# A transformer kernel on one core: the scheduler's stated step durations for DVE, ACT and PE set to measured ones

## The chip, the cores and the metric

The kernel runs on one core of one Trainium2 chip. A core has five engines that run in parallel, each through its own list of instructions in order: TensorE (PE, matrix products; PEld is its loading of weights), VectorE (DVE), ScalarE (ACT), GpSimd (POOL) and SyncE (SP, which here only issues DMAs). They wait for one another by semaphores. The metric is the device time of one execution in microseconds (us); lower is better.

## The reference

The program is two transformer blocks on 512 tokens of width 1024, in float32. The first has two layers, each with a mixer and a SwiGLU feed-forward part (width 2816), with RMS norms before and after. Layer 0 mixes by dilated band attention (12 heads), layer 1 by a gated DeltaNet (6 heads, forward and backward in time); both attend to 256 memory tokens too. The second block has three mixers side by side (GLA, S5, NSA) and one output projection. Cut to what matters:

```python
for i in range(2):
    h = rms_norm(x, pre[i]);  mem_n = rms_norm(mem, mem_norm[i])
    mixed = attention(h, mem_n, ...) if i == 0 else deltanet(h, mem_n, ...)
    x = x + rms_norm(mixed, post[i])
    h = rms_norm(x, ffn_pre[i])
    gate, up = split(h @ w_gate_up[i])
    x = x + rms_norm((silu(gate) * up) @ w_down[i], ffn_post[i])
proj = rms_norm(x, g) @ w_in
x = x + concat(gla(proj), s5(proj), nsa(proj)) @ w_out

# inside deltanet, per head and direction, chunk after chunk:
v_new = u - w @ state
out   = (q * exp(g)) @ state + intra @ v_new
state = state * exp(g_last) + (k * exp(g_last - g)).T @ v_new
```

## The kernel before

**Products.** Each float32 product is made of three matmuls on halves: an operand A is split into a high part Ah, rounded by ACT, and a low part Al = A - Ah, made by DVE; `mm3` (L267) issues low x high, high x low and high x high (lines L271, L272, L273), for each of eight slices of 128 of the inner width. These three lines, with output `bk`, are most of PE's work; "fill matmuls" here means those of them that stand between other work.

**Weights.** `weight_stream` (L216) brings each piece of weights by a DMA on SP's queue (L207) into one of three raw buffers, ACT makes `wh` (L243) and DVE makes `wl` (L262); for some pieces ("aside") POOL makes `wl`. A raw buffer is free again after its `wl`.

**Stages.** At the start the tokens x and the memory are read in tiles of 128 rows (L318), normed (L336 to L346: ACT's sum of squares, DVE's `iss`, POOL's root `irs` L340, DVE's scaled `hs` L346), transposed by PE (`hT` L354) and split (`Xh` L384, `Xl` L386). Then come layer 0's attention, whose last steps broadcast weights by PE (`fbc` L764), scale the output `oT` on DVE (L769) and split it for the output projection (`Xh` L794, `Xl` L796); its feed-forward part; layer 1's DeltaNet; its feed-forward part; and the second block.

**DeltaNet.** For each head an inverse is made by products on 64 columns (up to L1566, result `Uf` L1571). Then two chains, forward and backward, go over four chunks (`chain`, L1580): PE multiplies the state `St` (L1594), DVE makes `rhs` (L1597), PE multiplies by `Uf` (L1602), ACT reads `vn` (L1605), DVE scales it to `vs` (L1610), PE multiplies `vs` (L1612), DVE makes the next `St` (L1616, the first one by a copy L1619); outputs are two matmuls (L1624, L1625) and go to `otok`. When a head's two chains have ended, its output is normed (ACT L1651, POOL L1658), transposed (`poT` L1335), gated (`oT` L1661), and split for the projection (L1706, L1708).

**The order of the work** is made while the program is built, by a small list scheduler, `Flow` (L52 to L148). Every stage is written as threads, Python generators that yield an engine and a stated duration for each step and then issue its instructions. `Flow.start` gives the time at which a step could begin: when its engine is free and its inputs are there, plus `HOP` = 0.2 us where an input comes from another engine. `Flow.run` takes the step that could begin first; among those of the same engine that could begin within 0.1 us it takes the one with the lowest `late`. Tokens passed through `get` and `put` model the buffers. The stated durations are used for nothing else: they decide the order of instructions on each engine, and nothing at run time. Durations come from `act(n)` = 0.1 + 0.00084 n (L155), `dve(n)` = 0.07 + 0.00105 n (L159), `pool(n)` (L163), `MM` and `TR` (L152), or a number at the step:

```python
s = max(s, at + (self.HOP if e != eng else 0.0 if e == "PE" else 0.07))
```

Of the kernel before, what the change touches and what calls it, by code (L numbers as in the profile page):

```python
# [55 lines left out]
class Flow:  # L56
# [5 lines left out]

    HOP = 0.2

    def __init__(self, **sets):
# [33 lines left out]
    def run(self):  # L99
        while self.threads:  # L100
# [40 lines left out]
            s, t = min((x for x in ops if x[1]["req"][0] == t["req"][0] and x[0] <= s + DELTA), key=lambda x: x[1]["late"])  # L141
            eng, cost = t["req"][:2]
            self.free[eng] = s + cost
            t["tok"] = (s + cost, eng)
# [18 lines left out]
class K:  # L163
# [132 lines left out]
    def inputs(self, F, W, eX, eM, eF, pro):  # L296
# [93 lines left out]
        def memory():  # L390
            yield "late", 0.5
            for l in range(2):
                yield "wait", *eN[l]
                for c in range(2):
                    ev = W["mk"][l][c]
                    yield "wait", ev
                    yield "get", "mm"
                    p = self.psum("mm")
                    w = ev["W"]
                    for k in range(KT):  # L400
                        t = yield "PE", 0.33
                        self.mm3(p[:, :256], (w.h[:, k, :], w.l[:, k, :]), (M[l].h[:, k, :], M[l].l[:, k, :]),
                                 k == 0, k == KT - 1)
                    F.put("wsl", t)
                    F.add(evac(self.memK[l][:, c, :], p), 0.5, t)
                yield "wait", *W["mv"][l]
                for u in range(2):
                    yield "get", "mm"
                    p = self.psum("mm")
                    ts = slice(u * P, (u + 1) * P)  # L410
                    for k in range(KT):
                        w, kk = W["mv"][l][k // 4]["W"], k % 4
                        t = yield "PE", 0.33
                        self.mm3(p[:, :256], (M[l].h[:, k, ts], M[l].l[:, k, ts]), (w.h[:, kk, :], w.l[:, kk, :]),
                                 k == 0, k == KT - 1)
                    F.add(evac(self.memV[l][:, u, :], p, l == 1 and u == 1), 0.5, t)
                for _ in range(2):
                    F.put("wsl", t)
# [120 lines left out]
    def attention(self, F, W, eX, eM, eB, at, e2):  # L539
# [41 lines left out]
        def group(g):  # L581
# [37 lines left out]
            for i, t0 in enumerate((0, 64, 192, 320, 384)):  # L619
                yield "get", "mm"  # L620
                p = self.psum("mm")
                for k in range(KT):
                    w, kk = W2[k // 4]["W"], k % 4
                    t = yield "PE", 0.33
                    self.mm3(p[:, :256], (X.h[:, k, t0:t0 + P], X.l[:, k, t0:t0 + P]), (w.h[:, kk, :], w.l[:, kk, :]),
# [396 lines left out]
    def out_ffn(self, F, i, W, gnext, groups, kev, before):  # L1022
# [57 lines left out]
        for part, (f0, f1) in enumerate(self.PARTS):  # L1080
# [22 lines left out]
            while f < nf:  # L1103
                fs = (f, f + 1) if part == 0 and f == 0 else (f,)
                banks = {}
                for hv in ((0, 256), (256, 512)) if len(fs) == 2 else ((0, 512),):
# [3 lines left out]
                    for f_ in fs:  # L1110
                        for z in range(2):
# [6 lines left out]
                            for k in range(KT):  # L1118
                                tk = yield "PE", 0.65 * (t1 - t0) / 512
                                self.mm3(p[:, t0:t1], (ev["W"].h[:, k, :], ev["W"].l[:, k, :]),  # L1120
# [649 lines left out]
    def proj(self, F, ev, eX, m=P):  # L1770
# [7 lines left out]
        for t0, t1 in rngs:  # L1778
            yield "wait", *eX[t0 // P:t1 // P]
            for k in range(KT):  # L1780
                t = yield "PE", 0.65 * (t1 - t0) / S
                self.mm3(p[:m, t0:t1], (W.h[:, k, :], W.l[:, k, :]), (X.h[:, k, t0:t1], X.l[:, k, t0:t1]),
# [5 lines left out]
    def projector(self, F, items, eX, eP, late=20, haste=0):  # L1788
# [9 lines left out]
        def part(it, t0, t1):  # L1798
            W, m = it["W"], it["args"][4]
            yield "wait", *eX[t0 // P:t1 // P]  # L1800
            for k in range(KT):
                t = yield "PE", 0.65 * (t1 - t0) / S
                self.mm3(it["p"][:m, t0:t1], (W.h[:, k, :], W.l[:, k, :]), (X.h[:, k, t0:t1], X.l[:, k, t0:t1]),
# [15 lines left out]
        for i, it in enumerate(items):  # L1819
# [13 lines left out]
            for u in range(4):  # L1833
# [4 lines left out]
                for k in range(KT):  # L1838
                    W, kk = it[k // 4]["W"], k % 4
                    t = yield "PE", 0.33  # L1840
                    self.mm3(p[:, :256], (X.h[:, k, sl], X.l[:, k, sl]), (W.h[:, kk, :], W.l[:, kk, :]),
# [394 lines left out]
    def s5(self, F, W, eX, open_, eY, uT):  # L2236
# [140 lines left out]
        def glu():  # L2377
# [14 lines left out]
            for c in range(2):  # L2392
                zs = []
                for o in (2, 0):
# [3 lines left out]
                    for k in range(2):  # L2398
                        t = yield "PE", 0.65
                        self.mm3(p, (w.h[:, k, os_], w.l[:, k, os_]), yh[k], k == 0, k == 1)  # L2400
# [898 lines left out]
```

## Time and profile before

| | us |
|---|---|
| median of 3 runs (1761.16 to 1765.25) | 1763.18 |
| the profiled execution | 1761.48 |
| its span, first to last instruction | 1759.5 |
| PE busy | 1708.7 (97%) |
| DVE busy | 979.8 (56%) |
| ACT busy | 763.2 (43%) |
| POOL busy | 338.0 (19%) |

The profile is of one execution. An engine's busy time is the time in which it had an instruction in work, waits not counted; PE's matmuls overlap, so two that start 0.23 us apart may each be shown 0.4 us long. In a timeline a row gives the start, the length, the engine, the line of the kernel, the operation, output <- inputs, the size and a count xN of like instructions drawn together; in brackets stands how long the engine had been idle before it, and which instruction released it. Order listings, below, show the instructions of one engine in program order and hold no times.

### The profile page before, as it was taken

Reading aid. Unit: us, or ns where it says so; the run is one execution under the profiler, and the core shown is the slowest. Engines: PE = TensorE matmul, PEld = TensorE weight load, DVE = VectorE, ACT = ScalarE, POOL = GpSimd, SP = SyncE. Lnnn points to the kernel's source line nnn. Section 1 sums busy time; section 2 is a strip of 40 time slices with the busy share of each in tenths; the row PEclk is TensorE's granted clock in tenths of the full one; section 3 lists DMA queues with packets and bytes.
Section 4 is the critical chain, followed back from the end, with each engine's and each line's share of the span. In section 5 each row is a group of like instructions: output and inputs, shape, how many; then the busy total and the mean of one; then the engine's idle time right before and its main releaser. Section 6 shows DMA issues by size and latency. Waiting matters only on the chain.

```text
span 1759.5 us, 30190 instructions
## 1 busy us (share of the span) xinstructions
PE 1708.7 (97%) x12031; PEld 1423.2 (81%) x12031; DVE 979.8 (56%) x1997; ACT 763.2 (43%) x1808; POOL 338.0 (19%) x496
## 2 busy tenths in 40 slices
PE   6999999999999999999999899999999999999999
PEld 5988679888888888788777788888888888888787
DVE  6333656323333378867887467464433468467573
ACT  5443635333223245656555355333223353345671
POOL 5200001000000021220222351364540033210000
PEclk9999999999999999999999999999999999999999
DMA  6513133333233332211110164345333253552012
GB/s 195 154 51 95 49 120 97 120 96 96 96 96 96 96 114 79 61 38 38 38 37 32 59 152 139 109 133 144 108 108 96 77 159 115 153 154 69 25 37 84
DMA packets 211981, 167.84 MB, mean 95 GB/s; under 512 B 21996, under 2 KB 183036, under 8 KB 211840
## 3 DMA queue, kind: packets, MB, share of 16 engines
q1 hardware_dynamic: 203808, 154.39, 29.7%
q0 software_dynamic: 4560, 9.42, 2.1%
q10 hardware_dynamic: 3472, 2.10, 0.4%
q8 instruction: 94, 1.54, 0.4%
q14 instruction: 47, 0.39, 0.1%
HBM read 152.23 MB, written 13.65 MB: 94 GB/s over the span
## 4 chain that ended last, share of the span: by engine, by line
PE 84%; DVE 9%; ACT 2%; issue 2%; DMA 1%; POOL 1%; ACTq 0%; SPq 0%; DVEq 0%; POOLq 0%
PE bk L271 23%; PE bk L272 22%; PE bk L273 22%; DVE hn L1324 2%; DVE wl L262 1%; PE no L2753 1%; PE npT L2736 1%; PE x L1519 1%; PE x L1523 1%; PE y L1544 1%; DVE hs L942 1%; PE ns L2722 1%; PE hT L949 1%; PE ns L2720 1%; PE o L1625 1%
## 5 line engine op out<-in xcount | busy, mean ns | idle before, releaser
L262 DVE TENSOR_TENSOR wl<-raw,wh 128x512 fp32r<-128x512 f32 x450 | 315.8, 742 | 372.4 <-ACT wh L243 371.8
L243 ACT ACTIVATE wh<-raw 128x512 fp32r<-128x512 f32 x474 | 273.0, 623 | 534.4 <-PE bk L273 300.4
L271 PE MATMUL bk<-Xh,wl 128*128 128x512 f32 (+2 forms) x1312 | 494.9, 377 | 0.2 <-ACT Xh L951 0.2
L272 PE MATMUL bk<-Xl,wh 128*128 128x512 f32 (+2 forms) x1312 | 478.4, 365 | 0.5 <-DVE Xl L956 0.5
L273 PE MATMUL bk<-Xh,wh 128*128 128x512 f32 (+2 forms) x1312 | 478.5, 365 | 0.0
L273 PEld LDWEIGHTS bk<-Xh,wh 128*128 128x128 f32 (+1 forms) x1312 | 246.9, 188 | 40.1
L271 PEld LDWEIGHTS bk<-Xh,wl 128*128 128x128 f32 (+1 forms) x1312 | 247.5, 189 | 39.0 <-issue 3.5
L272 PEld LDWEIGHTS bk<-Xl,wh 128*128 128x128 f32 (+1 forms) x1312 | 247.7, 189 | 34.8 <-DVE Xl L956 0.9
L271 PE MATMUL bk<-wh,Xl 128*128 128x512 f32 (+1 forms) x424 | 152.6, 360 | 6.7 <-DVE Xl L796 3.7
L272 PE MATMUL bk<-wl,Xh 128*128 128x512 f32 (+1 forms) x424 | 145.8, 344 | 0.3 <-DVE wl L262 0.2
L273 PE MATMUL bk<-wh,Xh 128*128 128x512 f32 (+1 forms) x424 | 145.2, 342 | 0.0
L271 PE MATMUL bk<-wh,Al 128*128 128x512 f32 x352 | 139.7, 397 | 0.0
L272 PE MATMUL bk<-wl,Ah 128*128 128x512 f32 x352 | 139.5, 396 | 0.0
L921 POOL TENSOR_TENSOR nc<-ncm,nhalf 128x1 f32<-128x1 f32 x16 | 11.5, 720 | 661.9 <-DVE ncm L919 661.9
L273 PE MATMUL bk<-wh,Ah 128*128 128x512 f32 x352 | 138.6, 394 | 0.0
L1093 DVE TENSOR_TENSOR sg<-sg,bk 128x512 f32<-128x512 f32 x44 | 30.2, 687 | 124.7 <-PE bk L273 120.2
L271 PEld LDWEIGHTS bk<-wh,Xl 128*128 128x128 f32 x424 | 84.7, 200 | 18.0 <-DVE Xl L796 3.1
L273 PEld LDWEIGHTS bk<-wh,Xh 128*128 128x128 f32 x424 | 84.8, 200 | 8.1
L272 PEld LDWEIGHTS bk<-wl,Xh 128*128 128x128 f32 x424 | 85.0, 200 | 7.6 <-DVE wl L262 1.0
L271 PEld LDWEIGHTS bk<-wh,Al 128*128 128x128 f32 x352 | 66.0, 188 | 16.1
L273 PEld LDWEIGHTS bk<-wh,Ah 128*128 128x128 f32 x352 | 66.0, 188 | 16.0
L272 PEld LDWEIGHTS bk<-wl,Ah 128*128 128x128 f32 x352 | 66.1, 188 | 15.4
(586 smaller groups left out, 2623.8 us busy)
## 6 DMA issues: line engine op xcount, KB each, us to landing
raw<-in_ffn_w_gate_up_dram SPq DMA_DIRECT2D x88, 512.0 KB, 3.9
raw<-in_ffn_w_down_dram SPq DMA_DIRECT2D x44, 512.0 KB, 3.3
raw<-in_dn_w_in_dram SPq DMA_DIRECT2D x27, 512.0 KB, 4.0
raw<-in_att_w_in_dram SPq DMA_DIRECT2D x20, 512.0 KB, 4.1
raw<-in_w_in_dram SPq DMA_DIRECT2D x20, 512.0 KB, 3.8
raw<-in_mem_w_kv_dram SPq DMA_DIRECT2D x8, 512.0 KB, 3.6
raw<-in_att_w_out_dram SPq DMA_DIRECT2D x8, 512.0 KB, 3.3
xd<-x SPq DMA_DIRECT2D x8, 512.0 KB, 2.6
```

The lines of the kernel that those rows point to most:

```text
L243: nc.scalar.activation(wh[:, sl], ev["raw"][:, sl], AF.Copy)
L262: eng.tensor_tensor(wl[:, sl], raw[:, sl], wh[:, sl].bitcast(F32), op=OP.subtract)
L271: mm(out, A[1], B[0], start=first, stop=False, **kw)
L272: mm(out, A[0], B[1], start=False, stop=False, **kw)
L273: mm(out, A[0], B[0], start=False, stop=last, **kw)
L942: nc.vector.scalar_tensor_tensor(hh[:, hv[i]], x[:, t, hv[i]], r2, r["gain"][:, hv[i]], op0=OP.mult, op1=OP.mult)
L949: nc.tensor.transpose(p[:, k * P:(k + 1) * P], hh[:, i * 512 + k * P:i * 512 + (k + 1) * P], self.ident)
L1093: nc.vector.tensor_tensor(sg, sg, pu, op=OP.mult)
L1324: nc.vector.scalar_tensor_tensor(acc[:, d0:d1], raw[:, d0 + o:d1 + o], cw[:, ti, tap:tap + 1], acc[:, d0:d1], op0=OP.mult, op1=OP.add)
L1519: nc.tensor.matmul(dn8(b[i])[at], lhsT, rhs, start=True, stop=True)
L1523: nc.tensor.transpose(b[d][:, o:o + P], U[:, d, 2 * n:2 * n + 2, :].rearrange("p c q -> p (c q)"), self.ident)
L1544: nc.tensor.matmul(dn8(ys[par])[HB[f], d, n, :], T[d][HB[par], n, f, :], xs[f][HB[par], d, n, :], start=True, stop=True)
```

## The change

`Flow` adds a fixed amount to the stated duration of every step on DVE (0.08 us) and on ACT (0.07 us). The steps that issue one `mm3` state 0.36 us in the place of 0.33 for 256 columns, and 0.682 in the place of 0.65 for 512. No instruction's arithmetic changes: each engine issues the same instructions in another order, apart from loads of ACT's function tables, which follow from the order of ACT's functions: there are 7 where there were 11. In the new file lines are one or two further down. Of the eight places with a PE number two are shown.

```diff
@@ -61,6 +61,7 @@
 
 
     HOP = 0.2
+    STEP = {"DVE": 0.08, "ACT": 0.07}
 
     def __init__(self, **sets):
         self.free = dict.fromkeys(("PE", "ACT", "DVE", "POOL", "DMA"), 0.0)
@@ -140,6 +141,7 @@
             s, t = min(ops, key=lambda x: x[0])
             s, t = min((x for x in ops if x[1]["req"][0] == t["req"][0] and x[0] <= s + DELTA), key=lambda x: x[1]["late"])
             eng, cost = t["req"][:2]
+            cost += self.STEP.get(eng, 0.0)
             self.free[eng] = s + cost
             t["tok"] = (s + cost, eng)
             self.step(t, t["tok"])
@@ -398,7 +400,7 @@
                     p = self.psum("mm")
                     w = ev["W"]
                     for k in range(KT):
-                        t = yield "PE", 0.33
+                        t = yield "PE", 0.36
                         self.mm3(p[:, :256], (w.h[:, k, :], w.l[:, k, :]), (M[l].h[:, k, :], M[l].l[:, k, :]),
                                  k == 0, k == KT - 1)
                     F.put("wsl", t)
...
@@ -1116,7 +1118,7 @@
                                 banks[f_, z] = self.psum("bk"), nm
                             p = banks[f_, z][0]
                             for k in range(KT):
-                                tk = yield "PE", 0.65 * (t1 - t0) / 512
+                                tk = yield "PE", 0.682 * (t1 - t0) / 512
                                 self.mm3(p[:, t0:t1], (ev["W"].h[:, k, :], ev["W"].l[:, k, :]),
                                          (X.h[:, k, t0:t1], X.l[:, k, t0:t1]), k == 0, k == KT - 1)
                             if t1 == S:
...
```

**POOL at the start.** `irs` is the root of a tile's norm (two memory tiles, then four x tiles), `wl` the low half of memory weights, `rb` and `oh` are small inputs. Before:

```order
L340 TENSOR_TENSOR irs<-iss,nhalf 128x1 x2
L444 MEMSET rb 33x12
L446 DMA oh<-in_bucket_oh_dram 33x1152
L448 DMA rb<-in_rel_bias_dram 32x12
L340 TENSOR_TENSOR irs<-iss,nhalf 128x1
L262 TENSOR_TENSOR wl<-raw,wh 128x512 x3
L340 TENSOR_TENSOR irs<-iss,nhalf 128x1
L262 TENSOR_TENSOR wl<-raw,wh 128x512 x2
L340 TENSOR_TENSOR irs<-iss,nhalf 128x1
L262 TENSOR_TENSOR wl<-raw,wh 128x512 x2
```

After:

```order
L342 TENSOR_TENSOR irs<-iss,nhalf 128x1 x2
L446 MEMSET rb 33x12
L448 DMA oh<-in_bucket_oh_dram 33x1152
L450 DMA rb<-in_rel_bias_dram 32x12
L342 TENSOR_TENSOR irs<-iss,nhalf 128x1 x3
L264 TENSOR_TENSOR wl<-raw,wh 128x512 x2
L342 TENSOR_TENSOR irs<-iss,nhalf 128x1
L264 TENSOR_TENSOR wl<-raw,wh 128x512 x2
```

Before, each of the x tiles' `irs` stands behind a group of `wl` steps, three long at first; now three `irs` steps come one after the other ahead of the first `wl` steps. On SP's queue the four x tiles are now fetched one after the other, while before the third and the fourth stood behind pieces of weights; in PE's order the first transposes of x stand behind 24 memory matmuls where there were 45, the last behind 48 where there were 123.

**PE at the end of attention.** `ao` is the attention's output, `fbc` the broadcast of the groups' weights, `bk` the fill matmuls. Before:

```order
L706 MATMUL ao<-pT,V_882 64x128 x4
L764 MATMUL fbc<-ident,amx 64x128 x6
L271 MATMUL bk<-wh,Xl 128x512
L272 MATMUL bk<-wl,Xh 128x512
L273 MATMUL bk<-wh,Xh 128x512
L271 MATMUL bk<-wh,Xl 128x512
L272 MATMUL bk<-wl,Xh 128x512
L273 MATMUL bk<-wh,Xh 128x512
L764 MATMUL fbc<-ident,amx 64x128 x18
```

After:

```order
L273 MATMUL bk<-wh,Xl 128x512
L274 MATMUL bk<-wl,Xh 128x512
L275 MATMUL bk<-wh,Xh 128x512
L273 MATMUL bk<-wh,Xl 128x512
L274 MATMUL bk<-wl,Xh 128x512
L275 MATMUL bk<-wh,Xh 128x512
L273 MATMUL bk<-wh,Xl 128x512
L274 MATMUL bk<-wl,Xh 128x512
L275 MATMUL bk<-wh,Xh 128x512
L766 MATMUL fbc<-ident,amx 64x128 x12
L273 MATMUL bk<-wh,Xl 128x512
L274 MATMUL bk<-wl,Xh 128x512
```

Before, six broadcasts stand right behind the `ao` matmuls, then six fill matmuls, then the other eighteen, and the output projection. Now twelve fill matmuls stand behind the `ao` matmuls (the first three just ahead of the rows shown), and the twelve last broadcasts behind them, followed by 129 fill matmuls up to the projection's later steps, where there were 123.

**PE in the last head of DeltaNet**, in the middle of its two chains; `chain`, `o` and the names in them are those of the code, the numbers tell buffers apart. Before:

```order
L1594 MATMUL chain<-St_9699,kTh 128x128
L1624 MATMUL o<-St_9664,qe_9081 128x128
L1625 MATMUL o<-vn_9693,AT_9055 128x128
L271 MATMUL bk<-wh,Xl 128x512
L272 MATMUL bk<-wl,Xh 128x512
L273 MATMUL bk<-wh,Xh 128x512
L1602 MATMUL chain<-rhs_9715,Uf 128x128
L1594 MATMUL chain<-St_9710,kTh 128x128
L271 MATMUL bk<-wh,Xl 128x512
L272 MATMUL bk<-wl,Xh 128x512
L273 MATMUL bk<-wh,Xh 128x512
L1602 MATMUL chain<-rhs_9729,Uf 128x128
```

After:

```order
L1596 MATMUL chain<-St_9737,kTh 128x128
L1596 MATMUL chain<-St_9742,kTh 128x128
L1604 MATMUL chain<-rhs_9751,Uf 128x128
L1604 MATMUL chain<-rhs_9753,Uf 128x128
L1614 MATMUL chain<-vs_9761,ktok 128x128
L1614 MATMUL chain<-vs_9763,ktok 128x128
L1626 MATMUL o<-St_9737,qe_9143 128x128
L1627 MATMUL o<-vn_9757,AT_9070 128x128
L1626 MATMUL o<-St_9742,qe_9255 128x128
L1627 MATMUL o<-vn_9759,AT_9229 128x128
```

Before, blocks of three fill matmuls stand between the chains' links: from the last head's inverse (the last L1566) to its transposes `poT` there are 54 in all, 6 ahead of the first link, 33 in eleven blocks between the links, and 15 behind the last link. Now there are none from the inverse to `poT`, and the two chains' links stand side by side. All 54 stand ahead of that inverse now: counted from the start of the program, fill matmuls ahead of the six heads' inverses are 9, 15, 36, 45, 48 and 54 more than before.

## Rows read from the trace of the kernel before

**Rows 1.** The page's busy times: engine, us, share of the span, instructions.

```profile
PE 1708.7 (97%) x12031; PEld 1423.2 (81%) x12031; DVE 979.8 (56%) x1997; ACT 763.2 (43%) x1808; POOL 338.0 (19%) x496
```

**Rows 2.** Busy time by stretches: start:end, length, each engine's busy time, PE's clock, DMA.

```profile
core 0: us, PE busy (x) PEld busy (x) DVE busy (x) ACT busy (x) POOL busy (x), PEclk, DMA share, GB/s
0.00:45.00 45.00, 30.46 (x173) 26.00 (x174) 28.34 (x41) 25.79 (x48) 25.64 (x33) 0.92 0.66 193
200.00:240.00 40.00, 33.02 (x281) 24.64 (x280) 30.00 (x75) 21.52 (x72) 0.00 (x0) 0.96 0.09 28
700.00:740.00 40.00, 38.18 (x500) 29.80 (x499) 32.07 (x67) 25.72 (x59) 11.35 (x9) 1.00 0.20 54
740.00:844.70 104.70, 104.11 (x1276) 84.96 (x1274) 77.61 (x187) 60.13 (x169) 19.66 (x18) 1.00 0.16 42
844.70:983.00 138.30, 130.22 (x1716) 107.57 (x1716) 107.74 (x243) 75.70 (x214) 34.83 (x28) 0.98 0.12 36
983.00:998.80 15.80, 15.80 (x106) 13.92 (x104) 9.38 (x28) 5.35 (x16) 0.00 (x0) 1.00 0.00 1
998.80:1010.00 11.20, 8.05 (x34) 6.10 (x33) 3.45 (x7) 3.96 (x15) 8.70 (x13) 0.90 0.38 126
1010.00:1410.00 400.00, 399.16 (x1876) 331.48 (x1875) 205.91 (x424) 143.08 (x277) 149.83 (x288) 1.00 0.42 119
1470.00:1730.00 260.00, 258.06 (x2155) 213.03 (x2154) 166.95 (x372) 135.16 (x369) 28.44 (x30) 1.00 0.32 91
```

**Rows 3.** Timeline of the start: start, length, engine, line, operation, [idle before <- releaser].

```profile
21.06 0.68 DVE L262 TENSOR_TENSOR wl<-raw,wh 128x512 fp32r<-128x512 f32 x1
...
22.16 5.24 POOL L262 TENSOR_TENSOR wl<-raw,wh 128x512 fp32r<-128x512 f32 x3
...
27.94 2.29 DVE L346 SCALAR_TENSOR_TENSOR hs<-xs,irs,rowx 128x1024 f32<-128x1024 f32 x1 [0.52 <-POOL irs L340]
...
29.58 0.50 SPq L318 DMA_DIRECT2D xs<-in_x_dram  x1
...
30.37 1.07 PE L354 MATMUL hT<-ident,hs 128*128 128x128 f32 x8 [2.34 <-DVE hs L346]
```

**Rows 4.** Timeline of the end of attention.

```profile
229.83 2.19 PE L764 MATMUL fbc<-ident,amx 128*64 128x128 f32 x36
...
231.81 2.37 DVE L769 TENSOR_TENSOR oT<-oT,fbc 128x384 f32<-128x384 f32 x3
...
234.86 0.50 PE L271 MATMUL bk<-wh,Xl 128*128 128x512 f32 x1 [2.84 <-DVE Xl L796]
```

**Rows 5.** Timeline of DeltaNet's last head, its gate and the projection behind it.

```profile
981.66 0.47 PE L1566 MATMUL y<-xT 64*64 64x64 f32 x16
...
983.56 0.60 PE L1602 MATMUL chain<-vtok,Uf 128*128 128x128 f32 x4
...
986.11 0.38 PE L1594 MATMUL chain<-St,kTh 128*128 128x128 f32 x2
...
986.47 0.47 PE L271 MATMUL bk<-wh,Xl 128*128 128x512 f32 x1
...
986.53 0.35 DVE L1597 SCALAR_TENSOR_TENSOR rhs<-chain,neg,vtok 128x128 f32<-128x128 f32 x1 [0.26 <-PE chain L1594]
...
987.25 0.38 PE L1602 MATMUL chain<-rhs,Uf 128*128 128x128 f32 x2
...
988.16 0.28 DVE L1610 TENSOR_SCALAR vs<-vn,ksc 128x128 f32<-128x128 f32 x1
...
988.63 0.39 PE L1612 MATMUL chain<-vs,ktok 128*128 128x128 f32 x2
...
989.16 0.34 DVE L1616 SCALAR_TENSOR_TENSOR St<-St,etot,chain 128x128 f32<-128x128 f32 x1
...
998.65 0.39 PE L1625 MATMUL o<-vn,AT 128*128 128x128 f32 x2
...
1003.40 0.66 PE L1335 MATMUL poT<-ident,otok 128*128 128x128 f32 x4 [0.92 <-POOL otok L1658]
...
1006.28 0.50 PE L271 MATMUL bk<-wh,Xl 128*128 128x512 f32 x1 [2.23 <-DVE Xl L1708]
```

More of the change, by code (lines that the diff above doesn't have):

```diff
@@ L412, in memory @@
                         w, kk = W["mv"][l][k // 4]["W"], k % 4
-                        t = yield "PE", 0.33
+                        t = yield "PE", 0.36
                         self.mm3(p[:, :256], (M[l].h[:, k, ts], M[l].l[:, k, ts]), (w.h[:, kk, :], w.l[:, kk, :]),
@@ L623, in group @@
                     w, kk = W2[k // 4]["W"], k % 4
-                    t = yield "PE", 0.33
+                    t = yield "PE", 0.36
                     self.mm3(p[:, :256], (X.h[:, k, t0:t0 + P], X.l[:, k, t0:t0 + P]), (w.h[:, kk, :], w.l[:, kk, :]),
@@ L1780, in proj @@
             for k in range(KT):
-                t = yield "PE", 0.65 * (t1 - t0) / S
+                t = yield "PE", 0.682 * (t1 - t0) / S
                 self.mm3(p[:m, t0:t1], (W.h[:, k, :], W.l[:, k, :]), (X.h[:, k, t0:t1], X.l[:, k, t0:t1]),
@@ L1801, in part @@
             for k in range(KT):
-                t = yield "PE", 0.65 * (t1 - t0) / S
+                t = yield "PE", 0.682 * (t1 - t0) / S
                 self.mm3(it["p"][:m, t0:t1], (W.h[:, k, :], W.l[:, k, :]), (X.h[:, k, t0:t1], X.l[:, k, t0:t1]),
@@ L1839, in projector @@
                     W, kk = it[k // 4]["W"], k % 4
-                    t = yield "PE", 0.33
+                    t = yield "PE", 0.36
                     self.mm3(p[:, :256], (X.h[:, k, sl], X.l[:, k, sl]), (W.h[:, kk, :], W.l[:, kk, :]),
@@ L2398, in glu @@
                     for k in range(2):
-                        t = yield "PE", 0.65
+                        t = yield "PE", 0.682
                         self.mm3(p, (w.h[:, k, os_], w.l[:, k, os_]), yh[k], k == 0, k == 1)
```

## The prediction

> **What bounds the kernel now.** I read the profile's busy line first, then the busy time by stretches, then the timeline round the few places where TensorE (PE) stands still. The busy line says that PE is busy 97% of the span and the next engine, DVE, 56% [rows 1]: whatever an edit does to DVE, ACT or POOL, it moves the time only where PE then waits, or no longer waits. The busy time by stretches says where that can be. In the feed-forward part of the second layer PE is busy 399.16 of 400 us and in the second block 258.06 of 260, so nothing can be gained there by another order. What PE loses it loses in four stretches: 14.5 us in the first 45, 7.0 between 200 and 240, 10.5 between 700 and 983, and 3.15 in the 11.2 us that end DeltaNet [rows 2]. The change is a new order, and no instruction is added but scalar-table loads (7 in the place of 11, counted in the order; ACT is busy 143.08 of 400 us in the stretch that has most of them [rows 2]). So the sum is one of stalls of PE in those four places.
>
> Whether the new numbers are truer can be read too. The planner had a DVE step on 512 columns at 0.07 + 512 x 0.00105 = 0.61 us; the trace has 0.68 [rows 3], and the new figure is 0.69. But the planner also adds 0.2 us whenever a step waits for another engine, and in the trace a chain's matmul starts 0.19 us after the end of the DVE step that feeds it (988.16 + 0.28 = 988.44, then 988.63 [rows 5]). So its chains of short steps over several engines were nearly right, and now come out longer than they run: it will put more other work between their links.
>
> **Start, 0 to 45 us.** All four x tiles are now fetched one after the other, and POOL does the three small `irs` steps together, ahead of `wl` steps. Before, three `wl` steps took POOL from 22.16 to 27.40, the next `irs` came behind them, `hs` began at 27.94 and the transposes of the second x tile at 30.37, after PE had stood still 2.34 us [rows 3]. Both of that tile's delays (POOL's queue, and x tiles behind weights in the DMA queue, the last at 29.58 [rows 3]) go. What is late next is the weights' own path: one `wl` is moved behind some five DVE steps of 0.68 us [rows 3], which frees its raw buffer up to 3.4 us later. The gain is 2.3 us at least if that path is no tighter, and at most 2.3 plus what the clock loses in the stretch: at a granted 0.92 of 2.4 GHz that is 0.08 x 45 = 3.6 [rows 2], together 5.9. The loss, with the raw buffer late and nothing gained, is 3.4. I take -1.5, nearer the stall that the row shows than either end, since only one of two waits for `hs` is sure to go. Between -5.9 and +3.4.
>
> **End of attention, 200 to 240 us.** Before, PE ran all `fbc` broadcasts and then stood still 2.84 us for `Xl` at 234.86: the last three `oT` steps, 2.37 us from 231.81, stood on DVE behind two `wl` steps [rows 4]. In the new order twelve fill matmuls come between the `ao` matmuls and the broadcasts, and on DVE two of the `oT` steps stand ahead of the splits. At 0.227 us a matmul (the change's 0.682 for three) the twelve cover 2.7 us. I take -2.5: the stall of 2.84 less a short rest. At best the clock's dip goes too, 0.04 x 40 = 1.6 [rows 2], which makes -4.5; at worst the stretch after the broadcasts is bare as before and the twelve were taken from a place where they hid something, +1.5 (half the stall).
>
> **DeltaNet, 700 to 1010 us.** This is the largest piece, and its sign is open. The last head's two recurrences, forward and backward, are a chain of matmul, DVE, matmul, ACT, DVE, matmul, DVE. Before, 54 matmuls of a projection stood in the tail, from the last head's inverse to its transposes `poT`; now none stand there, and all 54 are ahead of that inverse. Bare, a step of the chain takes 0.77 us (`St` matmul at 986.11 to the end of `rhs` at 986.88) + 1.19 (987.25 to the end of `vs` at 988.44) + 0.87 (988.63 to the end of `St` at 989.50) + three handovers of 0.19 = 3.40 [rows 5]. A first step without its head, 1.19 + 0.19 + 0.87 + 0.19 = 2.44, two whole steps, 6.80, and a last one that ends with `vn` and the output, about 1.87 (0.77 + 0.19 + the matmul's 0.39 + `vn`, estimated at 0.5 with its handover), make 11.1 us from the first `Uf` matmul to the last output. It is 15.1 now, 983.56 to 998.65, of which PE was busy all the time [rows 2, 5]. Of those 15.1, 33 fill matmuls are 11 blocks of 0.78 each (986.47 to 987.25 [rows 5]) = 8.6, which leaves 6.5 of the chain's own work: the bare chain stalls 11.1 - 6.5 = 4.6. Ahead of it, from the last inverse at 981.66 (0.47 long) to 983.56, 1.4 us were covered and are not now. Behind it, from the chain's last output to the transposes `poT`, 999.04 to 1003.40 [rows 5], ends with 0.92 us of waiting, and the 15 fill matmuls that covered 3.5 of it are gone, so I count the whole 4.4 as bare. The wait behind `poT`, 2.23 [rows 5], had no cover and has none. Together 4.6 + 1.4 + 4.4 + 2.2 = 12.6 against the 3.15 of now: +9.5. Two things come back. There are twelve block changes fewer, each 0.78 - 0.682 = 0.1: -1.2. And the 54 matmuls, 54 x 0.227 = 12.3 us of work, stand earlier. Where they meet a hole they cost nothing. The order says how many more stand ahead of each head's inverse than before, and the rows give the holes there: nine up to the first inverse (2.0 us; 1.8 us of holes from 700 to 740), 27 more up to the third (6.1 us; 0.6 of holes up to 844.7), 18 more up to the last (4.1 us; 8.1 of holes up to 983) [rows 2]. That makes at most 1.8 + 0.6 + 4.1 = 6.5 by place. I take 4.5, since a hole and a fill in the same stretch need not meet. The term is 9.5 - 1.2 - 4.5 = +3.8. Its ends are +8.3, if none of the early fill meets a hole, and, if the heads' own links move so that all 10.5 us of holes are filled, 9.5 - 1.2 - 10.5 = -2.2.
>
> **Everything else.** Outside the tail PE has about ten changes of block fewer (298 blocks of fill before, 276 now, 12 of the 22 counted above), at 0.1 us: -1.0. In the feed-forward parts and the second block PE is without holes, so 0, with 2 us either way for the second block's new order.
>
> **The sum.** -1.5 - 2.5 + 3.8 - 1.0 = -1.2 against the profiled execution, 1761.48 us (its span of 1759.5 and 2 us around it): 1760.3. The median of the runs, 1763.18, is 1.7 above that execution, so the forecast for a median is 1762.0: 0.07% below, which is no change that can be told (a measurement of this kernel tells about 0.2%, 3.5 us).
>
> **The rivals.**
> B, the tail of DeltaNet decides. The planner keeps its 0.2 us handover on top of the true durations, so it feeds fill to chains that need less than it believes, and is out of fill at the last head, the one place where nothing else can cover. For it: half of the moved fill stands where 0.6 us of holes are [rows 2]. Against it: the 8.1 us of holes from 844.7 to 983. If no hole takes the early fill, the term is 9.5 - 1.2 = +8.3, and the clock, 0.90 in the 11.2 us after the chain [rows 2], could fall as far over the chain: 0.1 x 16 = 1.6. With -1 for the start, -1 for attention and 0 for the rest that is +7.9: about 1771. It decides when less than 1 us of the early fill meets holes; up to 4 us it still makes the kernel slower than it was.
>
> C, the holes are bigger than they look. A PE whose busy time is 104.11 of 104.70 us could still have room, if a busy matmul is one that waits in the array: weight loads take 84.96 of those (0.81) and 107.57 of the next 138.30 (0.78), while in the tail, dense with fill, they take 13.92 of 15.8 (0.88) [rows 2]. If what is missing is room, 0.07 x 104.7 and 0.10 x 138.3 make 21 us, enough for all the early fill. Then 9.5 - 1.2 - 12.3 = -4.0 in DeltaNet, and with the other three terms -9.0: about 1754. Against it: transposes and short matmuls have fewer weight loads for their time, which makes the same ratio without any room. The Trainium skill has a rule for C: Perfetto Trace Analysis, section Identifying the Most-Contended Engine, says that matmul busy time misleads because matmuls are pipelined, and that weight-load busy time is the one to judge headroom by. By that rule the kernel's headroom is 19% and not 3% [rows 1]; the rows agree that the two differ, and cannot show which of them fill would find.
>
> D, the stalls change places. Each stall that goes is one that a wl step or a transfer takes over (POOL's and the DMA queue's turns at the start, the broadcasts at 229.83 [rows 4] that now come later), and DeltaNet gives back what it takes: 0, so 1763. For it: PE's work is the same to the instruction. Against it: the waits at 30.37 and 234.86 have a cause that is moved away.
>
> **Chances.** The forecast 0.40, with a range of its own of 1756 to 1767 (0.15 faster by over 0.2%, 0.24 the same, 0.01 slower); B 0.25 (0.22 slower, 0.03 the same); C 0.21 (0.20 faster, 0.01 the same); D 0.14 (0.10 the same, 0.04 slower). That makes 0.35 faster, 0.38 the same, 0.27 slower. With C's middle at 1754 and B's at 1771, a range of 1752 to 1770 leaves out the lower third of C and somewhat over the upper third of B, and no more than 2 in 10 in all.
>
> **What would show it.** The start is right if the transposes `hT` of x have no wait over 1 us; wrong if PE then waits for `wl` or raw weights. Attention is right if the wait for `Xl` at the output projection is under 1 us. DeltaNet is right if PE waits 10 to 14 us from the last head's inverse to the projection behind it, and the holes before that shrink by 4 to 5; if they shrink by none, B; if the heads before run through in less time by more than their holes, C. The feed-forward stretches should keep their length within 1 us; if one of them moves by more, the sum has left out a term, and the forecast is wrong for a reason that is not in it.

## The result, and the profile after

The changed kernel takes 1786.24 us (median of 4, 1785.80 to 1791.99) against 1763.59 of before: slower, ratio 1.0137, interval 1.0113 to 1.0161. The forecast, 1762.0 in a range of 1752 to 1770, was wrong. The profiled executions are 1786.56 and 1761.48 us, 25.1 apart.

The page's head and busy line of the changed kernel, against [rows 1]:

```profile
span 1784.8 us, 30190 instructions
...
PE 1711.5 (96%) x12031; PEld 1425.5 (80%) x12031; DVE 966.9 (54%) x1997; ACT 758.0 (42%) x1804; POOL 340.5 (19%) x496
```

PE has 2.8 us more of busy time and 22.5 us more of standing still (1784.8 - 1711.5 = 73.3, before 50.8). So nearly all of the loss is waits of PE. To see where, both traces are cut into four parts at PE instructions that both have: at the first `hT` transposes of the second layer's norm, at the end of the last `poT`, and at the first `hT` of the second block's norm. First before, then after (start:end, length, PE, PEld, DVE, ACT, POOL busy, PE's clock, DMA share, GB/s):

```profile
0.00:634.60 634.60, 612.64 (x3291) 511.32 (x3292) 272.16 (x474) 243.26 (x543) 43.93 (x69) 0.99 0.34 103
634.60:1004.05 369.45, 352.27 (x3990) 292.15 (x3988) 281.93 (x632) 205.12 (x550) 85.27 (x73) 0.99 0.18 51
1004.05:1404.26 400.21, 397.13 (x1859) 329.69 (x1859) 203.90 (x418) 142.01 (x274) 154.68 (x295) 1.00 0.42 120
1404.26:1759.50 355.24, 346.67 (x2895) 290.00 (x2893) 221.80 (x475) 172.79 (x441) 54.10 (x60) 1.00 0.34 99
```

```profile
0.00:639.91 639.91, 612.67 (x3295) 512.11 (x3296) 269.99 (x475) 243.37 (x543) 45.34 (x69) 0.99 0.34 103
639.91:1018.67 378.76, 353.66 (x3987) 292.56 (x3985) 274.70 (x631) 205.38 (x550) 85.15 (x73) 0.99 0.18 50
1018.67:1425.32 406.65, 399.73 (x1861) 331.84 (x1861) 201.11 (x419) 136.72 (x270) 155.17 (x295) 0.99 0.41 118
1425.32:1784.84 359.52, 345.47 (x2892) 289.02 (x2890) 221.06 (x474) 172.58 (x441) 54.81 (x60) 1.00 0.34 98
```

Length minus PE's busy time is its waiting. A few matmuls stand on the other side of a cut in the new order (3990 and 3987 in the second part). The front is 5.3 us longer (waits +5.3), DeltaNet 9.3 (waits +7.9), the norm and feed-forward part behind it 6.4 (+3.8), the second block 4.3 (+5.5). No part pays for all, and none got shorter. Now the stretches of [rows 2], as the changed kernel has them:

```profile
0.00:45.00 45.00, 30.63 (x176) 25.92 (x177) 27.74 (x43) 25.95 (x47) 24.64 (x33) 0.96 0.64 190
200.00:242.00 42.00, 32.89 (x298) 25.29 (x299) 30.46 (x75) 21.05 (x72) 0.00 (x0) 0.96 0.09 27
746.90:999.56 252.66, 242.30 (x3013) 198.76 (x3012) 181.65 (x430) 138.15 (x385) 57.49 (x49) 0.99 0.13 37
999.56:1013.50 13.94, 10.90 (x84) 9.09 (x84) 7.24 (x25) 3.49 (x13) 0.75 (x1) 1.00 0.01 3
1013.50:1021.00 7.50, 0.94 (x5) 0.55 (x5) 2.06 (x5) 1.91 (x9) 5.27 (x8) 0.81 0.19 68
...
1493.00:1755.00 262.00, 254.99 (x2131) 209.75 (x2131) 164.95 (x369) 133.21 (x365) 28.36 (x29) 1.00 0.32 89
```

The third line is DeltaNet from the first head's inverse to the last; before it was

```profile
740.20:981.66 241.46, 232.78 (x2968) 191.39 (x2968) 184.40 (x425) 135.83 (x381) 54.36 (x45) 0.99 0.13 39
```

It is 11.2 us longer and has more waiting, 10.4 us against 8.7, though by the order it took up 45 fill matmuls more (54 less the 9 ahead of the first inverse), 10.2 us of work; PE's busy time there is 9.5 us longer. So in sum nothing of that fill was hidden in the holes. Behind it the last head stands bare: 3.0 us of waits from its inverse through the chain, and 6.6 in the gate and the projection's first wait. The same places in the timeline, with two of the start, two more of the end of attention, one of the norm and three of the second block:

```profile
20.19 0.55 PE L273 MATMUL bk<-Mh,wl 128*128 128x256 f32 x1 [1.48 <-ACT Mh L374]
...
26.91 1.07 PE L356 MATMUL hT<-ident,hs 128*128 128x128 f32 x8 [1.13 <-DVE hs L348]
...
216.83 0.88 PE L766 MATMUL fbc<-ident,amx 128*64 128x128 f32 x12 [1.53 <-DVE amx L758]
...
232.81 0.72 PE L766 MATMUL fbc<-ident,amx 128*64 128x128 f32 x10
...
236.24 0.58 PE L273 MATMUL bk<-wh,Xl 128*128 128x512 f32 x1 [2.71 <-DVE Xl L798]
...
999.56 0.83 PE L1568 MATMUL y<-xT 64*64 64x64 f32 x16 [0.42 <-ACT xT L1532]
1000.85 0.46 PE L1604 MATMUL chain<-vtok,Uf 128*128 128x128 f32 x2 [0.46 <-DVE Uf L1573]
...
1013.09 0.39 PE L1627 MATMUL o<-vn,AT 128*128 128x128 f32 x2
...
1017.83 0.84 PE L1337 MATMUL poT<-ident,otok 128*128 128x128 f32 x4 [4.36 <-POOL otok L1660]
...
1020.90 0.80 PE L273 MATMUL bk<-wh,Xl 128*128 128x512 f32 x1 [2.23 <-DVE Xl L1710]
...
1059.48 1.97 PE L951 MATMUL hT<-ident,hs 128*128 128x128 f32 x8 [2.68 <-DVE hs L944]
...
1517.94 0.69 PE L2110 MATMUL gs<-ge 32*64 32x64 f32 x32 [1.62 <-POOL ge L2089]
...
1614.23 0.66 PE L2676 MATMUL ncsT<-ident,sqt 128*128 128x128 f32 x4 [1.34 <-ACT sqt L2670]
...
1629.49 0.51 PE L273 MATMUL glu<-yh,wl 128*128 128x512 f32 x1 [1.01 <-DVE wl L264]
```

The wait for `poT` was 0.92 [rows 5]; that for `Xl` at the end of attention, 2.84 [rows 4], is there as before; the last three lie where PE waited 0.6 us or less before.

### The profile page after: what moved, and what is told of

Read it like the earlier page. It is cut to its first block, busy times and chain, and to the rows that moved or that the text cites. A ratio compares the mean times of both kernels' runs of the same rounds, so it can differ in the third digit from the quotient of the medians.

```text
span 1784.8 us, 30190 instructions
## 1 busy us (share of the span) xinstructions
PE 1711.5 (96%) x12031; PEld 1425.5 (80%) x12031; DVE 966.9 (54%) x1997; ACT 758.0 (42%) x1804; POOL 340.5 (19%) x496
## 4 chain that ended last, share of the span: by engine, by line
PE 85%; DVE 8%; ACT 2%; POOL 2%; issue 1%; DMA 1%; ACTq 0%; DVEq 0%; POOLq 0%
PE bk L273 23%; PE bk L274 22%; PE bk L275 22%; DVE wl L264 1%; PE no L2755 1%; PE x L1521 1%; PE npT L2738 1%; PE y L1546 1%; PE x L1525 1%; POOL wl L264 1%; DVE x L927 1%; PE ns L2724 1%; DVE hs L944 1%; PE ns L2722 1%; DVE Xl L958 1%
## 5 line engine op out<-in xcount | busy, mean ns | idle before, releaser
L923 POOL TENSOR_TENSOR nc<-ncm,nhalf 128x1 f32<-128x1 f32 x16 | 11.2, 698 | 659.8 <-DVE ncm L921 655.0
```

## The experiments

Times are medians; each ratio is against runs of the kernel before that were made beside it (their medians lie between 1762.2 and 1763.6). The additions are those to DVE and ACT; "old" PE numbers are 0.33 and 0.65. Part lengths are from each run's one profiled execution, cut as above.

| run | additions DVE, ACT | us | ratio (95%) | front | DeltaNet | norm, FFN | second |
|---|---|---|---|---|---|---|---|
| before | none | 1763.6 | | 634.6 | 369.4 | 400.2 | 355.2 |
| changed | 0.08, 0.07, new PE | 1786.2 | 1.0137 (1.0113, 1.0161) | 639.9 | 378.8 | 406.7 | 359.5 |
| 1 | none, new PE | 1784.3 | 1.0123 (1.0108, 1.0138) | 637.7 | 370.8 | 401.8 | 369.6 |
| 2 | 0.08, 0.07 | 1799.7 | 1.0212 (1.0196, 1.0227) | 640.3 | 382.9 | 409.8 | 364.8 |
| 3 | 0.004, 0.0035 | 1780.7 | 1.0110 (1.0093, 1.0127) | 637.4 | 370.5 | 401.5 | 365.5 |
| 4 | -0.004, -0.0035 | 1768.9 | 1.0035 (1.0022, 1.0048) | 637.7 | 370.8 | 401.3 | 356.4 |
| 5 | engine's time alone | 1792.6 | 1.0171 (1.0156, 1.0186) | 638.9 | 383.3 | 407.4 | 360.7 |
| 6 | result's time alone | 1792.5 | 1.0169 (1.0152, 1.0186) | 641.4 | 383.0 | 402.9 | 361.9 |
| 7 | handover by engine, new PE | 1782.5 | 1.0113 (1.0098, 1.0128) | 634.5 | 371.3 | 400.1 | 374.6 |
| 8 | 0.084, 0.0735, new PE | 1793.1 | 1.0174 (1.0159, 1.0189) | 640.1 | 381.0 | 408.8 | 359.3 |
| 9 | 0.04, 0.035 | 1770.5 | 1.0046 (1.0032, 1.0061) | 632.6 | 375.7 | 405.6 | 354.8 |
| 10 | -0.04, -0.035 | 1777.9 | 1.0085 (1.0064, 1.0105) | 639.5 | 366.9 | 402.9 | 368.0 |
| 11 | 0.076, 0.0665, new PE | 1790.6 | 1.0144 (1.0119, 1.0168) | 646.3 | 384.4 | 403.1 | 358.3 |
| 12 | -0.0111, -0.0016 | 1763.6 | 1.0004 (0.9994, 1.0014) | 639.6 | 366.5 | 401.6 | 355.9 |
| 13 | 0.08, 0.07 in DeltaNet | 1778.9 | 1.0088 (1.0070, 1.0106) | 631.5 | 385.7 | 402.4 | 355.1 |
| 14 | 0.08, 0.07 ahead of it | 1768.3 | 1.0028 (1.0016, 1.0040) | 642.2 | 369.0 | 400.5 | 355.2 |
| 15 | 0.08, 0.07 behind it | 1775.8 | 1.0074 (1.0056, 1.0092) | 633.1 | 371.5 | 405.1 | 363.0 |
| 16 | -0.02, 0.0068 from DeltaNet on | 1764.8 | 1.0011 (1.0001, 1.0020) | 634.7 | 363.5 | 401.1 | 360.9 |
| 17 | -0.02, 0.0068 in DeltaNet | 1760.2 | 0.9993 (0.9983, 1.0004) | 633.0 | 364.4 | 404.5 | 355.1 |
| 18 | 17, and 0.04, 0.035 ahead | 1757.9 | 0.9977 (0.9968, 0.9985) | 634.2 | 362.4 | 404.6 | 355.0 |

How far a part's length can be trusted shows where several orders have a part in common. PE's order is the same in the front of before, 13, 15, 16 and 17, and that front takes 631.5 to 634.7 us: its waits are 21.8 to 22.3 us, its busy time 609.2 to 612.6. In the same way DeltaNet takes 369.0 to 371.5 (before, 14, 15), the norm and feed-forward part 400.2 to 402.4 (before, 13, 14), and the second block 355.0 to 355.2 (before, 13, 14, 17, 18). So 3 us in the front, or 2 in the two middle parts, say nothing of an order.

**1. The PE numbers alone.**

```diff
-    STEP = {"DVE": 0.08, "ACT": 0.07}
+    STEP = {}
```

> Only the PE numbers of the change (0.36 and 0.682), DVE and ACT as before. Theory M (the longer stated DVE and ACT steps make the planner see waits of PE that it fills too early): these numbers alone cost nothing, 1759 to 1767. Theory J (any change of the numbers shuffles the order, and the order before was a good draw): slower, 1770 to 1790. Theory P (the waits of PE in the planner's own timetable come out on the chip at about 0.45 of their size, as 73.8 to 123.5 us planned became 50.8 to 73.3 measured): planned waits 78.6 us, so 1763.5 + 0.45 x 4.8 = 1766.

1784.3: nearly the whole loss of the change, from a part of it that the theory of the long steps (M) holds harmless. Its loss is in other places, though: 14.3 us of it in the second block, where the changed kernel lost 4.3.

**2. The additions alone** (the eight PE numbers put back).

> Only the additions to DVE (0.08) and ACT (0.07), the PE numbers as before. M: all of the loss or a little more, 1784 to 1795. J: slower by an amount that can't be told, 1770 to 1795. P: planned waits 145.4 us, 1763.5 + 0.45 x 71.6 = 1796.

1799.7, more than the whole change. The two halves do not add: 21.5 and 36.9 make 58, the change costs 23. P is within 4 us here.

**3 and 4. Additions without meaning** (PE numbers put back).

```diff
-    STEP = {"DVE": 0.08, "ACT": 0.07}
+    STEP = {"DVE": 0.004, "ACT": 0.0035}
```

> An addition without meaning: 0.004 us on DVE, 0.0035 on ACT, a twentieth of the change, the PE numbers as before. M: a twentieth of the loss at most, 1762 to 1766. J: slower by 8 us or more, 1772 to 1790. P: planned waits 89.4 us, 1763.5 + 0.45 x 15.6 = 1770.5.

> The same without meaning the other way: 0.004 us off DVE steps, 0.0035 off ACT steps. M: nothing, 1761 to 1765. J: slower by 8 us or more, 1772 to 1790. P: planned waits 73.9 us, as before: 1763.5.

A twentieth of the addition costs 18 us, which is J's sign; the same with the other sign costs 6, between M's range and J's. The planner takes whichever step could begin first, so a difference of 4 ns can turn one choice round, and every later choice then stands on another timetable: PE's order leaves that of before at its 41st matmul in run 3 and at its 56th in run 4, of 12031. P, by which the waits in the planner's own timetable tell those on the chip, has a miss of 18 us at run 1, and one of 10 at run 3.

**5 and 6. The addition cut in two.** For 5 the engine is taken longer, but the result is ready as before; for 6 the other way round. The lines of 6, in the place of `cost += ...`:

```diff
+            late = self.STEP.get(eng, 0.0)
             self.free[eng] = s + cost
-            t["tok"] = (s + cost, eng)
+            t["tok"] = (s + cost + late, eng)
```

> The additions (0.08 DVE, 0.07 ACT) lengthen only the time for which the engine is taken; the result is ready for the next step as early as before; PE numbers as before. Theory D (counted twice: in the trace two DVE steps of 512 columns one behind the other take 1.29 us though one is 0.69 long, so the engine is taken for 0.60, as was stated before, and the last 0.08 are within the 0.2 us that the planner adds for a handover anyway; both halves of the addition are too much): slower, 1775 to 1790. Theory R (the added times are right and only the scatter of the orders shows): 1763 to 1781, as the two jitters. M without the halves: half the loss, 1772 to 1782.

> The other half: the result is ready 0.08 (0.07) us later, the engine is free as early as before; PE numbers as before. D: slower, 1775 to 1790, since the 0.2 us of handover already hold it. R: 1763 to 1781.

1792.6 and 1792.5: each half loses 29 us by itself, more than any jitter and more than any of the theories allowed. That speaks for additions that do more than draw another order, and for either half as enough.

**7. Handover by engine.**

```diff
-    HOP = 0.2
+    HOP = {"PE": 0.2, "DVE": 0.135, "ACT": 0.12, "POOL": 0.06}
```

> No addition to any step, but the handover by the engine that gives the result: 0.2 from PE, 0.135 from DVE, 0.12 from ACT, 0.06 from POOL, and the changed kernel's PE numbers. D: with every time as the trace has it (a DVE step of 512 columns 0.608 + 0.135 = 0.743 until PE can start, 0.69 + 0.05 in the trace) the order is no worse than before, 1753 to 1768. R: a draw like any other, 1763 to 1790.

1782.5. D expected no loss and is wrong here: the run's DeltaNet, 371.3, is like that of the orders without an addition, but the second block takes 374.6, the longest of all. In this run, stated times that are nearer to the trace didn't make a better order. It doesn't say whether the handover or the PE numbers lose: run 1, with the same PE numbers and the old handover, is as slow (1784.3), also by its second block, and the new handover was not run with the old PE numbers.

**8 and 11. The change with the two jitters on top.**

```diff
-    STEP = {"DVE": 0.08, "ACT": 0.07}
+    STEP = {"DVE": 0.084, "ACT": 0.0735}
```

> The whole change with the meaningless twentieth of the first jitter on top: 0.084 on DVE, 0.0735 on ACT. If the change shifts the middle of the orders' times as well as drawing another one (D): around the changed kernel, 1780 to 1805, not below 1778. If it is a draw alone (J): anywhere from 1763 to 1795, as likely below 1778 as above.

> The whole change less a twentieth: 0.076 on DVE, 0.0665 on ACT. D and K: near the other two with the whole change (1786, 1793), 1778 to 1800. J: as likely under 1778 as above.

1793.1 and 1790.6. Six orders with whole additions or one half of them (changed, 2, 5, 6, 8, 11) lie between 1786 and 1800, the seven with no addition, a negative one or one of 0.004 (before, 1, 3, 4, 7, 10, 12) between 1763 and 1784. The two groups don't overlap: their means are 1792 and 1774, so there is a shift of some 18 us, and a scatter of about 20 in the lower group, of which the order before is the best. By parts the means differ by 3.9 us in the front, 12.8 in DeltaNet, 5.1 in the norm and feed-forward part and -2.9 in the second block, while the second block makes most of the lower group's scatter (355.2 to 374.6). Most of the shift is DeltaNet's, then. With the new PE numbers alone the groups are close, 1784 and 1783 (1, 7) against 1786 to 1793: there a DeltaNet that is 10 us longer stands beside a second block that is 13 us shorter.

The tail of DeltaNet tells the orders apart without exception. Fill matmuls from the last head's inverse to `poT` are none in all eight orders with additions over DeltaNet (changed, 2, 5, 6, 8, 9, 11, 13), and 39 to 60 in the other twelve; the part takes 375.7 to 385.7 us in the eight, 362.4 to 371.5 in the twelve.

**9, 10 and 12. Other amounts**, as in 3.

> Half of the additions (0.04 DVE, 0.035 ACT), PE numbers as before. If the loss grows with the addition (D) beside a scatter of some 8 us: 1775 to 1793, between the orders without an addition (1763 to 1784, five so far) and the whole one (1800). If only the drawing of another order counts (J): anywhere from 1763 to 1800.

> Half of the additions with the sign turned (0.04 off DVE, 0.035 off ACT steps), PE numbers as before: stated shorter than an engine is taken in the trace. D, if the old numbers were the best ones: slower than the two jitters' middle of 1775, 1775 to 1790. If shorter stated steps keep the projection's work back for the end whatever the truth is (call it K, keeps back): 1755 to 1772. J: anywhere.

> A third jitter of the numbers before: 0.0111 off DVE steps, 0.0016 off ACT steps. D, J: 1763 to 1784 as the other orders without an addition, no nearer to 1763 than they. K: on the low side, 1760 to 1772.

Half of the addition costs 7.6 us, less than a twentieth did in run 3 and less than D's range; but its DeltaNet, with a bare tail, is 6.3 us longer than before. The loss does not grow evenly with the addition. Run 12 is at before's own time, as K had it, but run 10, where K should show most, came out at 1777.9, outside its 1755 to 1772: shorter steps are no rule either. Run 10's DeltaNet is short (366.9) and its second block long (368.0).

**13, 14 and 15. The additions in one part of the plan.** All have old PE numbers; for 13

```diff
-            cost += self.STEP.get(eng, 0.0)
+            cost += self.STEP.get(eng, 0.0) if 625 <= s < 935 else 0.0
```

and for the others `s < 625` and `s >= 935`.

> The additions (0.08 DVE, 0.07 ACT) only for steps that the plan starts between 625 and 935 us (DeltaNet's projections, heads and tail), PE numbers as before. If the loss sits in DeltaNet (the projection's matmuls are used up ahead of the last head, and its tail stands bare): tail waits of 6 to 8 us against 0.9, 1772 to 1782. If it is spread evenly over the program: 1766 to 1771.

> The additions only for steps planned ahead of 625 us (start, attention, first feed-forward part). DeltaNet's loss is then gone: 1764 to 1774, 2 to 5 us of it waits in attention and the norm behind it; a draw of DeltaNet with the old numbers can add up to 8.

> The additions only for steps planned from 935 us on (norm behind DeltaNet, second feed-forward part, second block); all ahead of it in the order before. 1765 to 1772: 2 us more waits in the norm's transposes and 2 to 5 in the second block.

15.6, 5.0 and 12.5 us (the last above its range): together 33.1 of run 2's 36.9. So the loss is nearly additive by part, and nearly half of it is made in DeltaNet. That part of run 13, and the waits at its end:

```profile
631.52:1017.18 385.66, 358.79 (x3990) 298.10 (x3988) 277.81 (x632) 207.22 (x550) 86.83 (x74) 0.96 0.17 49
```

```profile
PE poT L1337 <- POOL otok L1660: 4.4, 1, 4.4
PE bk L273 <- DVE Xl L1710: 2.6, 2, 2.2
PE chain L1614 <- DVE vs L1612: 1.3, 3, 0.5
```

The wait before `poT` is that of the changed kernel, 4.4 against 0.92. PE waits 26.9 us in DeltaNet, 9.7 more than before, and 6.2 of the 9.7 stand behind the last inverse, where all 54 fill matmuls are gone. The part is 16.2 longer: the rest goes with a granted clock of 0.96 against 0.99. In run 15 the losses behind are made by other waits (in all, times, longest):

```profile
PE hT L951 <- DVE hs L944: 5.2, 5, 2.7
PE npT L2738 <- ACT nP L2730: 2.8, 4, 1.2
PE nqT L2625 <- DVE nqd L2620: 1.9, 1, 1.9
```

The first is 2.4 in the same stretch before.

**16. A shorter DVE step from DeltaNet on.**

```diff
+    STEP = {"DVE": -0.02, "ACT": 0.0068}
...
+            cost += self.STEP.get(eng, 0.0) if s >= 625 else 0.0
```

> From 625 us of the plan on 0.02 off each DVE step and 0.0068 on each ACT step, the front as before. If longer stated steps make the loss, a slightly shorter one has none: 1755 to 1768. If any new order loses against the one before: 1768 to 1785.

1764.8: no loss in sum, but two that cancel. DeltaNet is 5.9 us shorter than before, the second block 5.7 longer.

**17 and 18. Parts put together.** 17 is 16 with `625 <= s < 935`; 18 has the half addition of run 9 for `s < 625` besides.

> 0.02 off each DVE step and 0.0068 on each ACT step for steps planned between 625 and 935 us alone, all else as before. If the parts add up: 5.8 us less in DeltaNet by the trace of the run that had it, the second block again 328.6 us: 1763.3 - 5.8 = 1757.5, 1755 to 1760. If a part's order hangs on what stands ahead of it in the plan and the gains don't carry over: 1763 to 1772.

> The same, and half of the additions (0.04 DVE, 0.035 ACT) ahead of 625 us, where the run with half of them was 2.0 us shorter up to the end of the first feed-forward part. If the parts add up: 1755.5, 1752 to 1760. If DeltaNet's order is drawn anew by the changed front: 1757 to 1775.

DeltaNet and second block of 18:

```profile
634.19:996.54 362.35, 348.44 (x3979) 290.12 (x3978) 277.17 (x632) 205.98 (x550) 83.00 (x73) 0.99 0.18 52
1401.11:1756.10 354.99, 346.46 (x2895) 290.01 (x2893) 221.98 (x475) 172.94 (x441) 54.13 (x60) 1.00 0.34 99
```

DeltaNet's gain carried over: 7.1 us shorter than before, with 13.9 us of waits against 17.2, and a second block as before. But 4.4 of it comes back in the norm and feed-forward part, since part of the gain is work that crossed the cut: DeltaNet has 11 matmuls fewer, the next part 11 more and 2.6 us more of busy time. Run 18 is faster than both kernels, ratio 0.9977 (0.9968 to 0.9985), 4.3 us; 17, at 0.9993 and just above its range, can't be told from before. Run 18's time lies in both of its ranges; that DeltaNet kept its gain is seen in the part's length. The front's gain of run 9, 2.0 us, was none: it is less than the same order's scatter, and PE waits 24.4 us in that front where it waits 22.0 before.

## Why the prediction was wrong

**The step that failed** most is "In the feed-forward parts and the second block PE is without holes, so 0, with 2 us either way for the second block's new order", and with it the -1.0 for everything else. A stretch in which PE hardly waits can hardly be won by another order, but it can be lost by one: 258.06 of 260 became 254.99 of 262. The norm and feed-forward part behind DeltaNet and the second block cost 10.7 us of the 25.1. Run 3, with nothing but a new drawing, lost 10.3 us in the second block alone. The sum priced only the places where the order was looked at, as if the rest stayed; the prediction's own sign for a term left out, a feed-forward stretch that moves by more than 1 us, was met (+6.4). Of some 26 us between forecast and result, this makes 11.7; the front makes 9.3 (+5.3 for -4.0) and DeltaNet 5.5 (+9.3 for +3.8).

The holes were also read too narrowly. The four stretches hold 35.2 of the 50.8 us in which PE stands still [rows 1, 2]; the other 15.6, of which 8.6 lie in the second block and 6.2 between 240 and 700 us, had no term. And the -1.0 was too much: PE's order has 274 blocks of fill before and 258 after, not 298 and 276, which leaves four outside the tail, or 0.4 us by the prediction's price.

**Start**, -1.5: the wait of 2.34 for the second x tile is 1.13, as the moved `irs` would have it, but a new one of 1.48 came ahead of it, and the stretch waits 14.4 us in the place of 14.5: nothing. One wait gave way to another, which is rival D's mechanism.

**End of attention**, -2.5: wrong. The wait for `Xl` begins where the broadcasts end, at 232.02 before [rows 4] and at 233.53 now. Fill that stands ahead of the broadcasts moves both ends of that wait and covers none of it: it was 2.84 us and is 2.71. A wait of 1.53 for `amx` came in. With the norms behind it the front has 5.3 us more of waits.

**DeltaNet**, +3.8: measured +9.3. The tail was nearly right: the gate 4.4 forecast and 4.36 measured, `Xl` 2.2 and 2.23; the bare chain took 12.6 us (1000.85 to 1013.48) where 11.1 was worked out, but with 3.0 us of waits, the one ahead of it included, where 6.0 were (4.6 + 1.4): PE was busy for 10.1 of the 12.6 us, and not for 6.5 of 11.1. In all 9.6 us of waits against the 12.6 forecast. What failed is the term that was to come back, -4.5 for fill that meets holes earlier: the holes from the first inverse to the last grew from 8.7 to 10.4. That is rival B's mechanism, and run 13 shows it alone: with no addition anywhere else DeltaNet's tail stands bare and the kernel is 15.6 us slower. B's +8.3 for DeltaNet is near the +9.3 measured; its price for the whole, 1771, was too low, because it left the rest of the program at zero too.

**Rival C** (room that the busy time hides) is out: 10.2 us of fill lengthened a stretch of 241.46 us by 11.2, and PE's busy time in it by 9.5. **Rival D** is right for the start, and failed with the sum for the rest.

**"Whether the new numbers are truer"** was read too quickly. 0.68 is one DVE record; two behind each other take 1.28:

```profile
1063.77 1.29 DVE L264 TENSOR_TENSOR wl<-raw,wh 128x512 fp32r<-128x512 f32 x2
1064.98 0.15 DVE L937 SCALAR_TENSOR_TENSOR ncm<-ncs 128x1 f32<-128x1 f32 x1
1065.05 1.28 DVE L264 TENSOR_TENSOR wl<-raw,wh 128x512 fp32r<-128x512 f32 x2
```

So the engine is taken for 0.60, which is what 0.07 + 512 x 0.00105 = 0.61 had said, and the record's last 0.08 overlap the next one; the 0.2 of handover covered them. The handover was misread too. The matmul at 988.63, 0.19 us behind its DVE step, stood behind another one on PE; where PE really waits for DVE, as in the changed kernel's bare chain, it starts 0.05 us after the record's end. Before, then after:

```profile
988.39 0.40 PE L1602 MATMUL chain<-rhs,Uf 128*128 128x128 f32 x2
988.63 0.39 PE L1612 MATMUL chain<-vs,ktok 128*128 128x128 f32 x2
```

```profile
1002.59 0.29 DVE L1612 TENSOR_SCALAR vs<-vn,ksc 128x128 f32<-128x128 f32 x1 [0.63 <-ACT vn L1607]
1002.93 0.49 PE L1614 MATMUL chain<-vs,ktok 128*128 128x128 f32 x2 [0.43 <-DVE vs L1612]
```

So a step of 128 columns hands over after 0.34 us, where the planner had 0.20 + 0.2 = 0.40 and now has 0.48. The additions are a double count. That this is why they lose is not shown. Run 7, which takes the double count out another way, still loses 19 us, but it has the new PE numbers, and these lose 21.5 by themselves.

**What stays open**: of the 18 us by which orders with additions are slower on average, DeltaNet makes 12.8, and there the planner hands out the fill ahead of the last head in every order that has them. For the norms, the feed-forward part and the second block only the waits are shown, and not which stated time makes them. And the PE numbers alone cost 21.5 us (run 1) and 19 with the other handover (run 7), most of it in the second block, where a jitter alone cost 10; two orders can't tell a redraw from a shift.

## What to carry to other kernels

Before a change of a list scheduler's numbers is judged, run it with a meaningless change of the same numbers: here 0.004 us on a step moved the time by 6 and 18 us, and a single order says nothing below that. A stretch in which an engine is 99% busy can hardly be won by a new order, but it can be lost, so it must not be priced at zero. Fill covers a wait only if it stands behind the step with which the wait begins, as at the end of attention here. Cut the trace into parts that all orders share and change the numbers of one part at a time; here the parts' losses nearly added up (33 of 37 us). Compare the waits of a part before its length: the same order's front differed by 3 us in length and by 0.5 in waits.

## What the runs showed of the hardware that was not expected

A wait of PE can cost more than its own length. In run 13 the granted clock over DeltaNet was 0.96 where it was 0.99 before, and of 16.2 us more only 9.7 are waits. It is no rule: in the changed kernel's second block 5.5 us more of waits came with 4.3 us more of length. In the changed kernel the clock was 0.81 over the 7.5 us of the gate, and the first matmul behind it took 0.80 us where it took 0.50 before [rows 5]. A DVE record on 512 columns is 0.08 us longer than the time for which it holds the engine, and a matmul that waits for a DVE step starts 0.05 us after that step's record ends.
